# A hybrid linear-attention trunk: dropping the accumulating DMA in the second mixer, and loading the block it adds to by a DMA of its own elsewhere

## The chip, the cores and the metric

The kernel runs on one core of one Trainium2 chip. A core has five instruction streams that run side by side: TensorE (PE: matrix products, with its weight loads listed as PEld), VectorE (DVE), ScalarE (ACT), GpSimd (POOL) and SyncE (SP, which here only issues DMAs). Sixteen DMA engines move data between the HBM and the on-chip memory SBUF; products land in the eight banks of PSUM. The metric is the device time of one launch in microseconds (us), lower is better.

## The reference, cut to what matters

The reference is a trunk of two pre-norm residual layers in float32 on 256 tokens of width 2048: layer 0 mixes tokens by an HGRN2 gated recurrence, layer 1 by gated linear attention (GLA). Each mixer shares one input projection with a cross-attention into 256 memory tokens, and each layer ends with a SwiGLU network of inner width 5632.

```python
for layer in range(DEPTH):                       # DEPTH = 2
    hn = _rmsnorm(h, norm_mix[layer])
    if layer % NUM_MIXERS == 0:
        y, xq = _hgrn2_mixer(hn, hgrn_w_in[j], lbs[j], hgrn_onorm[j])
    else:
        y, xq = _gla_mixer(hn, gla_w_in[j], gla_w_gk[j], gla_b_gk[j], gla_onorm[j])
    xa = _memory_attention(xq, mem_n, w_mem_kv[layer])
    h = h + jnp.concatenate([y, xa], axis=-1) @ w_out[layer]
    hn = _rmsnorm(h, norm_ffn[layer])
    gate, up = jnp.split(hn @ w_gate_up[layer], 2, axis=-1)
    h = h + (jax.nn.silu(gate) * up) @ w_down[layer]
```

Nearly all of the work is in the weight products: `hn @ w_in`, `@ w_out`, `@ w_gate_up` and `@ w_down`, with `mem_n @ w_mem_kv` ahead of them. Each weight is used once, so each is loaded once.

## The kernel before, in words

**A product in three passes.** Each float32 factor is split into a high part that the PE takes at full rate and a low part, the rest (`split`, L276). ACT writes the high part, DVE (or, for a few, POOL at L292) subtracts it from the value to get the low part. A product is then three matmuls: high by high, high by low, low by high.

**Seven products for eight.** The weights of a product come in pairs of 128-row blocks, and two column ranges c0 and c1 are done together, so a pair is a 2 by 2 block matrix. It is loaded into one tile `raw` of four quarters, 128 partitions by up to 512 columns each: quarters 0 and 3 are the two row blocks of c0, quarters 1 and 2 are the two row blocks of c1. `raw` has three buffers. A pair of kind "S" is multiplied by a Strassen-Winograd scheme with seven block products (`seven`, L427); a pair of another kind takes eight. For "S" the kernel needs sums of quarters: quarter 1 plus quarter 2, then that sum minus quarter 0 (first `tt`, L436), then quarters 2 and 3 each minus the result (second `tt`, L437). Quarter 0, and quarters 2 and 3, are split before those two instructions, and their outcomes after them.

**Who makes the first sum.** `load_pair` (L413) issues, on SP's queue, a DMA for quarters 1 and 2 together (c1) and then a DMA for quarters 0 and 3 together (c0). For an "S" pair it then issues a third DMA on POOL's queue, which reads the second row block of c1 from HBM again and adds it into quarter 1 (`accum_op=ALU.add`, L425). That DMA may start only when the first has landed, and the first `tt` waits for it.

**Stages, in order of time.** Memory keys and values (`m0`, `m1`), HGRN (its projections `hx`, then for each of three groups `hf` and `hv`), output projection (`wo`), feed-forward (`f` and `fd`), then GLA (`gx`, `gk0`, `gg00`, `gg01`, `gk1`, `gg10`, `gg11`), output projection and feed-forward again. `project_two` (L522) runs the pairs of a mixer, of `w_out`, of `w_mem_kv` and of the end of `w_down`; `project_halves` (L597) those of `w_gate_up`. In GLA a product is 384 columns wide (two heads of 192, or one of 384), so a quarter is 192 KB; elsewhere it is 512 columns and 256 KB. GLA has ten "S" pairs: one in each of the two `gk` products ("------S-") and two in each of the four `gg` products ("-----SS-"). Their `raw` tiles have the numbers 230, 237, 238, 245, 246, 254, 261, 262, 269 and 270; names such as `parts230a` in the trace are the split parts of such a tile.

**What sets the order.** In the feed-forward stage the order on PE, DVE and ACT is the order in which the program writes it (`Engine.kept`, L141 and L614), with evictions and transposes put in at due times. In the other stages a planner, which estimates how long instructions and transfers take, fixes each engine's order at build time; small pieces of work such as the scores of a chunk, transposes and the decays are handed to it between pairs (`later`, `step`). On the chip every engine then works through its list in that order: an instruction whose input is late holds up all that stand behind it on its engine. When a product is done, DVE adds up its seven or eight banks (`early`, L552, and L594).

Of the kernel before, what the change touches and what calls it, by code (L numbers as in the profile page):

```python
# [14 lines left out]
ALU = mybir.AluOpType  # L15
# [25 lines left out]
def trunk_kernel(ctx: ExitStack, tc: tile.TileContext, x, mem, norm_mix, norm_ffn, norm_mem,  # L41
# [125 lines left out]
    def held(behind, func, *args):  # L167

        for e, last in behind:
            e.hold = last  # L170
        return func(*args)
# [7 lines left out]
    def mark(key):  # L179
        while waiting and waiting[0][0] <= key:  # L180
            waiting.pop(0)[2]()
# [228 lines left out]

    TIMES = {"S": (1,) * 7, "O": (0, 2, 2, 2, 2, 0, 0), "H": (0, 2, 2, 2, 1, 0, 1)}

    def load_pair(raw, w, p, c0, c1, n, kind):  # L413

        if n_w[0] == 1:
            for k, j, c in ((0, 0, c0), (0, 1, c1), (1, 3, c0), (1, 2, c1)):
                nc.sync.dma_start(out=raw[:, j, 0:n], in_=w[(2 * p + k) * P:(2 * p + k + 1) * P, c:c + n])
                if k == 0 and c == c1:
                    load_mem(0, 256, 512)
            return  # L420
        for j, c in ((slice(1, 3), c1), (slice(0, 4, 3), c0)):
            nc.sync.dma_start(out=raw[:, j, 0:n],
                              in_=w[2 * p * P:(2 * p + 2) * P, c:c + n].rearrange("(k p) c -> p k c", p=P))
        if kind == "S":
            nc.gpsimd.dma_start(out=raw[:, 1, 0:n], in_=w[(2 * p + 1) * P:(2 * p + 2) * P, c1:c1 + n], accum_op=ALU.add)  # L425

    def seven(i, raw, between=None):  # L427

        n = raw.shape[2]
        tt = ve.tensor_tensor  # L430
        b00, = split(raw[:, 0:1, :], f"{i}a")
        b11, b10 = split(raw[:, 2:4, :], f"{i}b")
        if between:
            between()

        tt(out=raw[:, 0, :], in0=raw[:, 1, :], in1=raw[:, 0, :], op=ALU.subtract)  # L436
        tt(out=raw[:, 2:4, :], in0=raw[:, 2:4, :], in1=raw[:, 0:1, :].broadcast_to([P, 2, n]), op=ALU.subtract)  # L437
        t6, t7 = split(raw[:, 0:2, :], f"{i}c", turned=True)
        t5, t4 = split(raw[:, 2:4, :], f"{i}d")
        return {1: ("x00", b00), 2: ("x01", b10), 3: ("z", b11), 4: ("x11", t4), 5: ("s", t5), 6: ("u", t6), 7: ("d0", t7)}  # L440
# [79 lines left out]
            self.x = lambda k, t: quads[p // 2].x(p % 2 * 2 + k, t)  # L520

    def project_two(pairs, plan, w, c0, c1, n, name, give, view=lambda ps: ps, onto=None, prep=None, behind=None,  # L522
                    base=0):

        ps, out = {}, []  # L530
        if any(c.isdigit() for c in plan):
            order, plan = [base + int(c) for c in plan[::2]], plan[1::2]
        else:
            sevens, plains = iter(range(len(PAIRS))), iter(range(plan.count("S"), len(PAIRS)))
            order = [next(sevens if c == "S" else plains) for c in plan]
        left = {b: plan.count("S") * (b < 8) + 2 * plan.count("-") * (b in (2, 3, 4, 8)) for b in range(1, 9)}

        def product(b, left_factor, right):
            first = b not in ps
            if first:  # L540
                ps[b] = bank(f"{name}p{b}")
            left[b] -= 1
            (xh, xl), (hi, lo) = left_factor, right
            acc = ps[b][:, 0:n]
            pe.matmul(acc, xh, hi, start=first, stop=False)
            pe.matmul(acc, xh, lo, start=False, stop=False)
            pe.matmul(acc, xl, hi, start=False, stop=left[b] == 0)

        def add(to, b, other):
            ve.tensor_tensor(out=to, in0=view(ps[b][:, 0:n]), in1=other, op=ALU.add)  # L550

        def early():  # L552
            l, r = give()
            out.extend((l(0), l(1), r(0), r(1)))
            s0, s1, e1, e0 = out
            ac.copy(out=s0, in_=view(ps[1][:, 0:n]))
            add(e1, 6, s0)
            add(s1, 7, e1)
            add(e0, 5, s1)
            add(e1, 5, e1)  # L560
            if onto:
                for to, part in zip(onto, out):
                    ve.tensor_tensor(out=to, in0=to, in1=part, op=ALU.add)
                out[:] = onto

        for at, (p, kind) in enumerate(zip(order, plan)):
            i, raw = new_raw()
            if i == 0:
                load_pair(raw, w, p, c0, c1, n, kind)
            if prep:  # L570
                prep(at)
            if i > 0:
                load_pair(raw, w, p, c0, c1, n, kind)
            if kind == "S":
                todo = held(behind, seven, i, raw[:, :, 0:n]) if behind else seven(i, raw[:, :, 0:n])
                last = at == plan.rindex("S")
                for b in (1, 6, 7, 5, 2, 4, 3) if last else (3, 2, 1, 6, 7, 5, 4):
                    product(b, pairs[p].get(todo[b][0]), todo[b][1])
                if last and at == len(plan) - 1:
                    early()  # L580
                elif len(pending) > MANY:
                    step()
                continue
            b00, b01 = split(raw[:, 0:2, 0:n], f"{i}a", 2 if i else 1)
            b11, b10 = split(raw[:, 2:4, 0:n], f"{i}b")
            if at > 0 and at == plan.rindex("S") + 1:
                early()
            for k, (lf, rt) in enumerate(((b00, b01), (b10, b11))):
                step()
                for b, t, right_factor in ((2, 0, lf), (4, 1, lf), (8, 1, rt), (3, 0, rt)):  # L590
                    if b == 8 and len(pending) > MANY:
                        step()
                    product(b, pairs[p].x(k, t), right_factor)
        for to, b in zip(out, (2, 4, 3, 8)):  # L594
            add(to, b, to)

    def project_halves(forms, kinds, w, c0, c1, name, key, keep):  # L597


        left = {b: sum(TIMES[kind][b - 1] for kind in kinds) for b in range(1, 8)}  # L600
        ps = {}

        def product(b, left_factor, right):
            first = b not in ps
            if first:
                ps[b] = bank(f"{name}p{b}")
            left[b] -= 1
            (xh, xl), (hi, lo) = left_factor, right
            pe.matmul(ps[b], xh, hi, start=first, stop=False)
            pe.matmul(ps[b], xh, lo, start=False, stop=False)  # L610
            pe.matmul(ps[b], xl, hi, start=False, stop=left[b] == 0)

        for p, kind in enumerate(kinds):
            Engine.kept = keep <= p  # L614
            i, raw = new_raw()
            load_pair(raw, w, p, c0, c1, 512, kind)
            x = forms[p].get
            last = p == len(PAIRS) - 1
            if kind == "S":
                todo = seven(i, raw, lambda: mark(key + p))  # L620
                for b in (1, 2, 6, 7, 5, 4, 3) if last else (1, 3, 2, 6, 7, 5, 4):
                    product(b, x(todo[b][0]), todo[b][1])
            else:
                b00, b01 = split(raw[:, 0:2, :], f"{i}a")
                mark(key + p)
                b11, b10 = split(raw[:, 2:4, :], f"{i}b")
                todo = [[(2, "x00", b00), (5, "x10", b01), (4, "x10", b00), (3, "d0", b01)]]
                if kind == "O":
                    todo.append([(2, "x01", b10), (5, "x11", b11), (4, "x11", b10), (3, "d1", b11)])
                else:  # L630
                    ve.tensor_tensor(out=raw[:, 3, :], in0=raw[:, 3, :], in1=raw[:, 2, :], op=ALU.subtract)
                    e1, = split(raw[:, 3:4, :], f"{i}c")
                    todo.append([(2, "x01", b10), (3, "x01", b11), (7, "x11", b11), (4, "x11", e1)])
                todo = [m for ms in zip(*todo) for m in ms] if last else todo[0] + todo[1]
                for b, f, right in todo:
                    product(b, x(f), right)
            step()
        return ps
# [398 lines left out]
    def gla_pair(w, pr, dec, decay, hq, r, yq):  # L1037
# [40 lines left out]
        def give():  # L1078
            for name in "kq":
# [2 lines left out]
            return [lambda t, d=d: d[:, t, :, 0:DK] for d in dst]  # L1082

        project_two(hq["pairs"], ("------S-", "------S-")[pr], w, kw + pr * 2 * DK, pr * 2 * DK, 2 * DK, f"gk{pr}", give,
                    lambda ps: ps.rearrange("p (a c) -> p a c", c=DK))
        for d in dst:
            for t in range(NT):
                ac.activation(out=d[:, t, :, 0:DK], in_=d[:, t, :, 0:DK], func=AF.Copy, scale=r[:, t:t + 1])
# [7 lines left out]
        for a in range(2):  # L1096
            def give():
                for dst, tag in ((gate, "gate"), (v, "v")):
# [1 line left out]
                return [lambda t, d=d[a]: d[:, t, :] for d in (gate, v)]  # L1100

            project_two(hq["pairs"], GLA[pr][a], w, 2 * kw + MIX + (2 * pr + a) * DV, 2 * kw + (2 * pr + a) * DV, DV,
                        f"gg{pr}{a}", give)
            for dst, func in ((gate[a], AF.Silu), (v[a], AF.Copy)):
                for t in range(NT):
                    ac.activation(out=dst[:, t, :], in_=dst[:, t, :], func=func, scale=r[:, t:t + 1])
# [288 lines left out]
```

## Time and profile before

| | |
|---|---|
| median of 3 runs | 2276.28 us (2270.11 to 2280.8) |
| the profiled execution | 2272.82 us, of it span 2271.0 us |
| granted TensorE clock | 0.999 |
| PE, PEld busy | 99%, 84% of the span |
| DVE, ACT, POOL busy | 87%, 63%, 9% |
| moved by DMA | 475.56 MB, 209 GB/s over the span |

A page of the profile has busy times by engine, the chain of work that ended last (followed back from the last instruction to what released each step), groups of equal instructions, and DMA issues with their size and the median time from issue to landing. A row of the timeline gives start, duration, engine, line, operation, `out<-in`, the number of instructions merged, and in brackets how long the engine had sat idle before it and what ended that. Matmuls are pipelined and their ends are modelled. Instructions of PE, DVE and ACT pass through one helper, so nearly all have line L151 and are told apart by their tiles.

### The profile page before, as it was taken

How to read it: one execution, taken by the hardware profiler on the slowest of the kernel's cores; microseconds unless marked ns; L12 is line 12 of the kernel's file. 1: busy time of each engine (PE TensorE's matmuls, PEld its weight loads, DVE VectorE, ACT ScalarE, POOL GpSimd, SP SyncE). 2: the span in 40 equal slices, each digit the busy share in tenths (PEclk: the TensorE clock that was granted, in tenths of full speed). 3: DMA queues.
4: the chain of work that ended last, by engine and by line, in shares of the span. 5: the costliest groups of instructions: out<-in, count | busy, mean ns of one | idle time of the engine just before them, and what ended most of it. 6: DMA issues, size and time to landing. Idle time of an engine off the chain costs nothing.

```text
span 2271.0 us, 30130 instructions
## 1 busy us (share of the span) xinstructions
PE 2247.5 (99%) x10710; PEld 1904.3 (84%) x10710; DVE 1974.3 (87%) x2449; ACT 1429.7 (63%) x1938; POOL 210.9 (9%) x215
## 2 busy tenths in 40 slices
PE   9999999999999999999999999999999999999998
PEld 7888888888888888888889899888888888888887
DVE  7889999898898889988996786789888898888997
ACT  7656656565666666666675565567566666666664
POOL 1000100000111111111100000000011111111110
PEclk9999999999999999999999999999999999999999
DMA  8656665656777777777765556466677777777774
GB/s 293 215 170 208 203 184 166 194 195 181 223 233 226 223 231 247 224 215 228 235 211 164 149 161 191 139 212 213 195 222 223 235 231 220 232 230 228 232 240 153
DMA packets 254827, 475.56 MB, mean 209 GB/s; under 512 B 15663, under 2 KB 46419, under 8 KB 254419
## 3 DMA queue, kind: packets, MB, share of 16 engines
q1 hardware_dynamic: 231203, 429.64, 56.1%
q0 software_dynamic: 22176, 39.72, 11.1%
q10 hardware_dynamic: 1296, 4.26, 0.5%
q8 instruction: 84, 1.38, 0.2%
q14 instruction: 68, 0.56, 0.1%
HBM read 470.42 MB, written 3.15 MB: 209 GB/s over the span
## 4 chain that ended last, share of the span: by engine, by line
PE 94%; DVE 2%; DMA 2%; issue 1%; ACT 0%; SPq 0%; POOL 0%; POOLq 0%; DVEq 0%; ACTq 0%
PE f_p L151 39%; PE fd L151 19%; PE wo L151 4%; PE m1p L151 2%; PE hv2p L151 2%; PE hv1p L151 2%; PE hv0p L151 2%; PE wo0p L151 2%; PE wo1p L151 2%; PE hf2p L151 2%; PE hf1p L151 2%; PE fd_0p L151 2%; PE m0p L151 2%; PE gg01p L151 1%; PE hf0p L151 1%; DMA raw<-in_gla_w_in_dram 1%
## 5 line engine op out<-in xcount | busy, mean ns | idle before, releaser
L151 DVE TENSOR_TENSOR raw<-raw 128x512 f32<-128x512 f32 (+3 forms) x320 | 299.0, 934 | 62.7 <-DMA raw<-in_w_gate_up_dram 34.0
L151 DVE TENSOR_TENSOR parts<-raw,parts 128x1024 fp32r<-128x1024 f32 (+1 forms) x196 | 224.3, 1179 | 23.4 <-ACT parts L151 23.0
L151 ACT CAST parts<-raw 128x1024 fp32r<-128x1024 f32 (+1 forms) x216 | 212.6, 1017 | 50.4 <-PE fd L151 6.5
L425 POOL DMA_DIRECT2D raw<-in_w_gate_up_dram x114 | 98.9, 867 | 990.2 <-DMA raw<-in_w_gate_up_dram 670.1
L151 ACT COPY h<-fd 128x512 f32<-128x512 f32 x80 | 46.6, 588 | 79.1 <-PE fd L151 75.8
L292 POOL TENSOR_TENSOR parts<-raw,parts 128x1024 fp32r<-128x1024 f32 x20 | 48.8, 2440 | 204.3 <-ACT parts L151 192.0
L151 ACT ACTIVATE s<-s,rf_r 128x512 f32<-128x512 f32 x44 | 31.8, 723 | 41.9 <-DVE s L151 41.7
L151 DVE TENSOR_TENSOR e<-f_p,e 128x512 f32<-128x512 f32 x66 | 45.3, 686 | 2.6 <-DVE s L151 0.5
L151 ACT COPY fd<-h 128x512 f32<-128x512 f32 x82 | 45.3, 585 | 0.0
L151 PE MATMUL fd<-parts,s_2h 128*128 128x512 f32 x128 | 39.8, 392 | 0.0
L151 PE MATMUL fd<-parts,s_0h 128*128 128x512 f32 x128 | 39.8, 392 | 0.0
L151 PE MATMUL fd<-parts,s_4h 128*128 128x512 f32 x128 | 39.8, 392 | 0.0
L151 PE MATMUL fd<-parts,s_8h 128*128 128x512 f32 x128 | 39.8, 392 | 0.0
L151 PE MATMUL fd<-parts,s_6h 128*128 128x512 f32 x128 | 39.8, 392 | 0.0
L151 PE MATMUL fd<-parts,s_3h 128*128 128x512 f32 x128 | 39.4, 389 | 0.0
L151 PE MATMUL fd<-parts,s_7h 128*128 128x512 f32 x128 | 39.4, 389 | 0.0
L151 PE MATMUL fd<-parts,s_5h 128*128 128x512 f32 x128 | 39.4, 389 | 0.0
L151 PE MATMUL fd<-parts,s_1h 128*128 128x512 f32 x128 | 39.4, 389 | 0.0
L151 DVE TENSOR_TENSOR s<-f_p,e 128x512 f32<-128x512 f32 x44 | 30.3, 690 | 10.1 <-PE f_p L151 8.2
L425 POOL DMA_DIRECT2D raw<-in_hgrn_w_in_dram x17 | 14.8, 872 | 216.0 <-DMA raw<-in_hgrn_w_in_dram 125.9
L151 DVE SCALAR_TENSOR_TENSOR s<-e,rf_r,s 128x512 f32<-128x512 f32 x44 | 31.0, 747 | 0.2
L151 PEld LDWEIGHTS fd<-parts,s_7h 128*128 128x128 f32 x128 | 24.0, 188 | 5.0
(5729 smaller groups left out, 7315.4 us busy)
## 6 DMA issues: line engine op xcount, KB each, us to landing
raw<-in_w_gate_up_dram SPq DMA_DIRECT2D x352, 512.0 KB, 4.2
raw<-in_w_down_dram SPq DMA_DIRECT2D x80, 1024.0 KB, 6.7
raw<-in_hgrn_w_in_dram SPq DMA_DIRECT2D x96, 512.0 KB, 4.2
raw<-in_gla_w_in_dram SPq DMA_DIRECT2D x96, 384.0 KB, 3.3
raw<-in_w_gate_up_dram POOLq DMA_DIRECT2D x114, 256.0 KB, 5.4
raw<-in_w_out_dram SPq DMA_DIRECT2D x16, 1024.0 KB, 5.2
raw<-in_w_out_dram SPq DMA_DIRECT2D x32, 512.0 KB, 4.1
raw<-in_w_mem_kv_dram SPq DMA_DIRECT2D x30, 512.0 KB, 5.6
```

The costliest lines, as they stand in the source:

```text
L151: ins = func(*args, **kwargs)
L292: low = (nc.gpsimd if free_port else ve).tensor_tensor(out=both[:, 1, k:j, 0:m], in0=src[:, k:j, :], in1=both[:, 0, k:j, 0:m].bitcast(F32) ...
L425: nc.gpsimd.dma_start(out=raw[:, 1, 0:n], in_=w[(2 * p + 1) * P:(2 * p + 2) * P, c1:c1 + n], accum_op=ALU.add)
```

## The change

`project_two` and `seven` get a flag `fed`, true by default, and GLA's two calls of `project_two` set it to false.

Where `fed` is false, an "S" pair has no accumulating DMA. Its load is the two DMAs on SP's queue, with c0 (quarters 0 and 3) now ahead of c1 (quarters 1 and 2), and `seven` adds quarter 2 into quarter 1 by one more DVE instruction in front of the two it had.

Where `fed` is true, an "S" pair has four DMAs instead of three: quarter 1 alone, the accumulating DMA on POOL's queue right behind it in the program, then quarters 0 and 3, then quarter 2 alone. Pairs of the other kinds keep two DMAs everywhere, with c0 now ahead of c1. The very first pair of the kernel is loaded as before.

```diff
-    def load_pair(raw, w, p, c0, c1, n, kind):
+    def load_pair(raw, w, p, c0, c1, n, kind, fed):
...
-        for j, c in ((slice(1, 3), c1), (slice(0, 4, 3), c0)):
-            nc.sync.dma_start(out=raw[:, j, 0:n],
-                              in_=w[2 * p * P:(2 * p + 2) * P, c:c + n].rearrange("(k p) c -> p k c", p=P))
-        if kind == "S":
-            nc.gpsimd.dma_start(out=raw[:, 1, 0:n], in_=w[(2 * p + 1) * P:(2 * p + 2) * P, c1:c1 + n], accum_op=ALU.add)
+        if kind == "S" and fed:
+            rows = [w[(2 * p + k) * P:(2 * p + k + 1) * P, c1:c1 + n] for k in range(2)]
+            nc.sync.dma_start(out=raw[:, 1, 0:n], in_=rows[0])
+            nc.gpsimd.dma_start(out=raw[:, 1, 0:n], in_=rows[1], accum_op=ALU.add)
+        nc.sync.dma_start(out=raw[:, 0:4:3, 0:n], in_=w[2 * p * P:(2 * p + 2) * P, c0:c0 + n].rearrange("(k p) c -> p k c", p=P))
+        if kind == "S" and fed:
+            nc.sync.dma_start(out=raw[:, 2, 0:n], in_=rows[1])
+        else:
+            nc.sync.dma_start(out=raw[:, 1:3, 0:n], in_=w[2 * p * P:(2 * p + 2) * P, c1:c1 + n].rearrange("(k p) c -> p k c", p=P))
...
-    def seven(i, raw, between=None):
+    def seven(i, raw, fed, between=None):
...
+        if not fed:
+            tt(out=raw[:, 1, :], in0=raw[:, 1, :], in1=raw[:, 2, :], op=ALU.add)
         tt(out=raw[:, 0, :], in0=raw[:, 1, :], in1=raw[:, 0, :], op=ALU.subtract)
...
         project_two(hq["pairs"], ("------S-", "------S-")[pr], w, kw + pr * 2 * DK, pr * 2 * DK, 2 * DK, f"gk{pr}", give,
-                    lambda ps: ps.rearrange("p (a c) -> p a c", c=DK))
+                    lambda ps: ps.rearrange("p (a c) -> p a c", c=DK), fed=False)
...
             project_two(hq["pairs"], GLA[pr][a], w, 2 * kw + MIX + (2 * pr + a) * DV, 2 * kw + (2 * pr + a) * DV, DV,
-                        f"gg{pr}{a}", give)
+                        f"gg{pr}{a}", give, fed=False)
```

More of the change, by code (lines that the diff above doesn't have):

```diff
@@ L522, in project_two @@
     def project_two(pairs, plan, w, c0, c1, n, name, give, view=lambda ps: ps, onto=None, prep=None, behind=None,
-                    base=0):
+                    base=0, fed=True):
         ps, out = {}, []
@@ L568, in project_two @@
             if i == 0:
-                load_pair(raw, w, p, c0, c1, n, kind)
+                load_pair(raw, w, p, c0, c1, n, kind, fed)
             if prep:
@@ L572, in project_two @@
             if i > 0:
-                load_pair(raw, w, p, c0, c1, n, kind)
+                load_pair(raw, w, p, c0, c1, n, kind, fed)
             if kind == "S":
-                todo = held(behind, seven, i, raw[:, :, 0:n]) if behind else seven(i, raw[:, :, 0:n])
+                todo = held(behind, seven, i, raw[:, :, 0:n], fed) if behind else seven(i, raw[:, :, 0:n], fed)
                 last = at == plan.rindex("S")
@@ L615, in project_halves @@
             i, raw = new_raw()
-            load_pair(raw, w, p, c0, c1, 512, kind)
+            fed = True
+            load_pair(raw, w, p, c0, c1, 512, kind, fed)
             x = forms[p].get
@@ L619, in project_halves @@
             if kind == "S":
-                todo = seven(i, raw, lambda: mark(key + p))
+                todo = seven(i, raw, fed, lambda: mark(key + p))
                 for b in (1, 2, 6, 7, 5, 4, 3) if last else (1, 3, 2, 6, 7, 5, 4):
```

## The prediction

> **What bounds the kernel now.** I read the page first (busy times, the chain that ended last, the DMA issues), then the busy times by stage, then the timeline of PE in the one stage where PE had gaps, and last the rows of DVE ahead of each gap.
>
> ```profile
> span 2271.0 us, 30130 instructions
> PE 2247.5 (99%) x10710; PEld 1904.3 (84%) x10710; DVE 1974.3 (87%) x2449; ACT 1429.7 (63%) x1938; POOL 210.9 (9%) x215
> ...
> PE 94%; DVE 2%; DMA 2%; issue 1%; ACT 0%; SPq 0%; POOL 0%; POOLq 0%; DVEq 0%; ACTq 0%
> ```
>
> PE is idle for 2271.0 − 2247.5 = 23.5 us in all. A change that leaves the matmuls alone, as this one does, can win no more than that. The rows by stage (window; length, then busy time of PE, PEld, DVE, ACT, POOL) say where these 23.5 us lie.
>
> ```profile
> 0.00:105.00 105.00, 101.51 (x475) 83.46 (x476) 80.96 (x116) 69.63 (x114) 9.43 (x13) 1.00 0.75 254
> ...
> 146.00:422.00 276.00, 275.98 (x1376) 232.72 (x1375) 260.30 (x358) 165.91 (x226) 19.91 (x22) 1.00 0.62 190
> ...
> 517.00:1164.00 647.00, 647.00 (x2904) 536.72 (x2903) 578.90 (x623) 417.81 (x516) 75.08 (x69) 1.00 0.74 226
> ...
> 1210.00:1484.00 274.00, 262.96 (x1601) 255.70 (x1600) 205.42 (x338) 160.74 (x257) 15.55 (x23) 0.99 0.56 166
> ...
> 1575.00:2222.00 647.00, 647.00 (x2904) 536.55 (x2903) 579.50 (x622) 418.61 (x517) 75.13 (x69) 1.00 0.74 226
> 2222.00:2271.00 49.00, 41.34 (x183) 33.91 (x181) 34.53 (x51) 21.94 (x35) 1.11 (x2) 0.97 0.43 151
> ```
>
> The HGRN groups (146 to 422) and both feed-forward stages have no PE gap at all. GLA (1210 to 1484) has 274.00 − 262.96 = 11.0 us, the largest part of the 23.5; of the rest 3.5 us lie at the start and 7.7 us at the end, where the last outputs are scaled and stored. So the change can win in GLA, and only there. Its PE gaps are these (the bracket is the idle time and what ended it):
>
> ```profile
> 1263.47 1.99 PE L151 MATMUL zp<-gk 128*128 128x256 f32 x8 [1.79 <-DVE gk L151]
> 1282.62 0.44 PE L151 MATMUL tgk<-ident,gsk 128*128 128x128 f32 x2 [1.03 <-ACT gsk L151]
> 1283.86 0.88 PE L151 MATMUL tgk<-ident,gsk 128*128 128x128 f32 x6 [0.80 <-ACT gsk L151]
> ...
> 1327.33 1.16 PE L151 MATMUL slg<-GQ 128*128 128x128 f32 x8 [2.34 <-DVE GQ L151]
> ...
> 1422.06 1.16 PE L151 MATMUL slg<-GQ 128*128 128x128 f32 x8 [2.39 <-ACT GQ L151]
> 1426.47 1.13 PE L151 MATMUL slg<-GQ 128*128 128x128 f32 x8 [1.15 <-DVE GQ L151]
> ...
> 1463.84 0.30 PE L151 MATMUL ty<-ident,ggate 128*128 128x128 f32 x1 [0.53 <-DVE gro_v L151]
> 1465.15 0.33 PE L151 MATMUL ty<-turned_id,ggate 128*128 128x128 f32 x1 [1.01 <-DVE ggate L151]
> ```
>
> They add up to 11.04 us, all of the stage's idle time.
>
> **GLA: what is removed.** Ten accumulating DMAs go. What they cost today is the idle time of DVE ahead of the first `tt` of a pair, the one that takes the sum. First the ten of them as a group (count, busy time, mean ns, idle time before them), then the ones that idled longest:
>
> ```profile
> L151 DVE TENSOR_TENSOR raw<-raw 128x384 f32<-128x384 f32 x10 | 5.6, 557 | 14.2 <-DMA raw<-in_gla_w_in_dram 10.1 <-issue 3.2 <-DVE parts237a L151 0.5
> ...
> 1255.19 0.51 ACT L151 CAST parts230a<-raw 128x384 fp32r<-128x384 f32 x1 [0.49 <-DMA raw<-in_gla_w_in_dram]
> 1260.45 0.56 DVE L151 TENSOR_TENSOR raw<-raw 128x384 f32<-128x384 f32 x1 [4.16 <-DMA raw<-in_gla_w_in_dram]
> ...
> 1262.99 0.42 DVE L151 COPY gk<-tlow 128x256 f32<-128x256 f32 x1
> ...
> 1410.70 0.56 DVE L151 TENSOR_TENSOR raw<-raw 128x384 f32<-128x384 f32 x1 [1.39 <-issue]
> ...
> 1418.13 0.56 DVE L151 TENSOR_TENSOR raw<-raw 128x384 f32<-128x384 f32 x1 [3.02 <-DMA raw<-in_gla_w_in_dram]
> ...
> 1457.89 0.56 DVE L151 TENSOR_TENSOR raw<-raw 128x384 f32<-128x384 f32 x1 [2.93 <-DMA raw<-in_gla_w_in_dram]
> ```
>
> Three of the PE gaps stand right behind these stalls. Pair 230: DVE stands still until 1260.45, and the copy of `gk` at 1262.99, for which PE waits at 1263.47, is behind it on DVE. Pairs 261 and 262: DVE idles 1.39 and 3.02 us, and the decays `GK` and `GQ`, for which PE waits at 1422.06 and 1426.47, are behind. Pair 269: DVE idles 2.93 us, and the normalisation `gro_v`, for which PE waits at 1463.84 and 1465.15, is behind.
>
> **GLA: what is added.** One DVE instruction for each of the ten pairs, two inputs and one output of 128x384 float32. The group above is this very kind of instruction: 557 ns, so 10 × 0.557 = 5.6 us of DVE time against 14.2 us of idle time that goes or shrinks. SP's count of DMAs stays, and c0 and c1 change places. The first work on a pair, the cast of quarter 0, needs c0, which now is in front; the new sum needs c1, which now comes last, at about the moment at which c0 came before. For pair 230 that is just before 1255.19, where ACT had waited for it; DVE was free from 1260.45 − 4.16 = 1256.29. So the sum starts at once and its data is no new wait.
>
> **GLA: the sum.** For each place: the stall that goes less the added instructions, but no more than the PE gap behind it.
> - Pair 230: 4.16 − 0.56 = 3.60 us saved on DVE, the gap is 1.79 us. Win 1.79.
> - Pairs 261 and 262: 1.39 + 3.02 − 2 × 0.557 = 3.30 us saved, the gaps are 2.39 + 1.15 = 3.54 us. Win 3.30.
> - Pair 269: 2.93 − 0.56 = 2.37 us saved, the gaps are 0.53 + 1.01 = 1.54 us. Win 1.54.
> - Pairs 237 and 238, ahead of the gap at 1327.33: nearly no stall there to remove (0.5 us, the group row's `parts237a`), two instructions added, 1.11 us. Of the 13 us ahead of that gap DVE idles in the two places below, 1.9 us together, and both times for an ACT result that itself follows on DVE's or PE's work, so between 0 and 1.11 us reaches PE. I take the middle, 0.55. Loss 0.55.
>
> ```profile
> 1314.11 1.23 DVE L151 TENSOR_TENSOR GF<-GF,ab 128x1024 f32<-128x1024 f32 x1 [1.11 <-ACT ab L151]
> ...
> 1318.45 0.96 DVE L151 TENSOR_TENSOR parts239a<-raw,parts239a 128x768 fp32r<-128x768 f32 x1 [0.77 <-ACT parts239a L151]
> ```
>
> - Pairs 245, 246 and 254: no gap behind them; hidden by PE, which has work ready there. If that cover were gone: 3 × 0.557 = 1.7 us.
> - The gaps at 1282.62 and 1283.86 are the adding up of the finished `gk` banks on DVE; no load is in front of it, so they stay.
>
> Together 1.79 + 3.30 + 1.54 − 0.55 = 6.1 us faster. Bounds: nothing is won below 0 if the loads are what DVE waits for (a rival, below); above, all eight gaps, 11.0 us.
>
> **Elsewhere: 144 pairs with one more DMA.** The issues (count, KB each, median us from issue to landing):
>
> ```profile
> raw<-in_w_gate_up_dram SPq DMA_DIRECT2D x352, 512.0 KB, 4.2
> raw<-in_w_down_dram SPq DMA_DIRECT2D x80, 1024.0 KB, 6.7
> ...
> raw<-in_w_gate_up_dram POOLq DMA_DIRECT2D x114, 256.0 KB, 5.4
> ...
> raw<-in_hgrn_w_in_dram POOLq DMA_DIRECT2D x17, 256.0 KB, 4.2
> ...
> raw<-in_w_out_dram POOLq DMA_DIRECT2D x6, 256.0 KB, 4.0
> ...
> raw<-in_w_down_dram POOLq DMA_DIRECT2D x4, 256.0 KB, 7.1
> ...
> raw<-in_w_mem_kv_dram POOLq DMA_DIRECT2D x3, 256.0 KB, 5.6
> ```
>
> 114 + 17 + 6 + 4 + 3 = 144 pairs. Two sizes give a line: 512 KB more cost 6.7 − 4.2 = 2.5 us, so a DMA has about 4.2 − 2.5 = 1.7 us that do not depend on its size, and 256 KB should land in 4.2 − 1.25 = 2.95 us. The accumulating DMA can thus start about 1.25 us earlier and the sum is there about that much earlier (as an estimate; between 0, if POOL is held up otherwise, and 4.2 − 1.7 = 2.5). This shortens waits of DVE that PE does not see: where PE has no gap, the gain is nothing. The cover is PE's queue of finished work, and it is deep:
>
> ```profile
> 904.65 0.69 DVE L151 TENSOR_TENSOR parts160a<-raw,parts160a 128x512 fp32r<-128x512 f32 x1 [2.82 <-ACT parts160a L151]
> ...
> 915.03 0.61 PE L151 MATMUL f_p<-parts160a,hf_0h 128*128 128x512 f32 x2
> ...
> L422 SPq DMA_DIRECT2D raw<-in_w_gate_up_dram x352: 367/368/1781, 496.1 to 2177.9; - x176
> ```
>
> DVE was done with `parts160a` at 905.34, PE took it at 915.03: 9.7 us of lead. On the other side of the ledger, quarter 2 now leaves last, one issue later than c0 did: 0.37 us by the last row, with the accumulating DMA perhaps beside it on the DMA engines. SP's queue gets 144 × 0.37 = 53 us of issue time spread over the span, and behind those issues stand only later loads. I take 0 us for all of this; the bounds are 0 for a gain (no PE gap to close) and the rival on the third DMA for a loss. Pairs of other kinds swap c0 and c1, but their first split takes quarters 0 and 1 together and so needs both DMAs, as before: 0.
>
> **The total.** 2272.82 − 6.1 = 2266.7 us for a run like the profiled one. That one stands 2276.28 − 2272.82 = 3.5 us below the median of the three runs, so the median after should be 2276.28 − 6.1 = 2270.2, rounded to 2270.
>
> **Rivals.**
> *Hidden anyway (the loads, not the accumulating DMAs, hold DVE).* If c1, now last, lands late, DVE waits at the new sum instead of at the old one. For: ACT itself waited for c0 of pair 230 until 1255.19. Against: DVE then stood 4.16 us longer. If two thirds of the stalls stay, 2 us are won: 2274.
>
> *All gaps close.* The planner decides GLA's order anew with ten late transfers gone and may put the adding up and the decays earlier; then up to 11.0 us: 2265. Against: the gaps at 1282.62 and 1327.33 hang on finished banks and on DVE's load, which gets 5.6 us more.
>
> *The planner's order gets worse.* Outside the feed-forward stages, changed estimates of 30 loads with four DMAs (HGRN, output, memory) and ten in GLA move DVE instructions. DVE is busy 260.30 of 276 us in HGRN, so there is little room. If one gap of the size at 1327.33 opens in each of the three groups and two more elsewhere, 5 × 2.34 = 11.7 us are lost against 6.1 won: 2282.
>
> *Slower: the third DMA's fixed 1.7 us is not overlapped.* The place is the feed-forward stages, whose DVE order is fixed: if quarter 2 lands late, the split of quarters 2 and 3 waits and all DVE work behind it. DVE has (647.00 − 578.90) + (647.00 − 579.50) = 135.6 us of idle time there, 1.19 us for each of the 114 pairs. From 1.19 us of lateness for each pair on, PE pays; at the full 1.7 us it is (1.7 − 1.19) × 114 = 58 us, so 2328 after the win in GLA. Against it: DMAs on one queue overlap. In GLA the two loads of pair 230 were both there by 1255.19, though each is 384 KB.
>
> On this the Trainium skill speaks against the change ("DMA: Bandwidth & Descriptors", section "Anatomy of one DMA — SWDGE (gpsimd) path"): a DMA, there one issued by GpSimd, has a constant part of about 2.0 us, mostly the wait until its last write is confirmed, so that many small ones cost more than few large ones. The 1.7 us worked out above agree. By that rule with nothing overlapped, the loss would be (2.0 − 1.19) × 114 = 92 us; the lead of PE and the overlapping loads are why I do not go by it.
>
> **How the numbers follow.** Chances: forecast (3.5 to 9 us won) 0.58; hidden anyway 0.16; all gaps close 0.09; worse order 0.12; third DMA 0.05. The runs of before spread over 2270.11 to 2280.8, about ±0.25% around the median, so less than 0.5% (11.4 us) can't well be told from no change; that is where "same" ends. Faster than 2264.9 needs nearly all gaps closed, or the forecast and a low draw of the runs: 0.12. Slower than 2287.7 needs the third DMA, or a worse order that loses half as much again: 0.07. The rest, 0.81, is the same. The range takes in the forecast, the first two rivals and the worse order with half the spread of the runs (about 4 us) at either end: 2260 to 2283; the third DMA is left out. The likeliest case alone would be 2264 to 2276.
>
> **What would show each step.** The profile after should have no accumulating DMA from `gla_w_in`, and 20 DVE instructions `raw<-raw` of 128x384 with an idle time before them of a few us instead of 14.2. The PE waits for `gk`, for `GQ` behind pairs 261 and 262 and for `gro_v` should be gone or under 0.5 us each; the wait for `GQ` near 1327 should be there still, perhaps longer; GLA's PE idle time should fall from 11.0 to about 5 us. The feed-forward stages should take 647 us as before with no PE gap, and DVE's waits for `gate_up` loads should shrink. I am wrong if GLA keeps its stalls at the new sum, if a feed-forward stage grows, or if HGRN shows PE gaps.

## The result, and the profile after

The changed kernel takes 2262.16 us (median of 6 runs, 2260.94 to 2262.71), the kernel before 2273.2 us (median of 6, 2270.11 to 2280.8). The ratio is 0.9943 with a 95% interval of 0.9933 to 0.9953: faster by 0.47 to 0.67%. The prediction said 2270 us (2260 to 2283), a win of 6.1 us; the win is 11.0 us by these medians.

The page of the changed kernel (span, busy times, chain that ended last), beside which the prediction's first fence stands for the kernel before:

```profile
span 2259.0 us, 30203 instructions
...
PE 2245.2 (99%) x10710; PEld 1903.1 (84%) x10710; DVE 1974.4 (87%) x2459; ACT 1425.3 (63%) x1938; POOL 202.3 (9%) x205
...
PE 94%; DVE 2%; issue 1%; DMA 1%; ACT 0%; SPq 0%; POOLq 0%; DVEq 0%; POOL 0%; ACTq 0%
```

The span is 12.0 us shorter, and PE idles 2259.0 − 2245.2 = 13.8 us instead of 23.5. Nearly all of this difference of 9.7 us lies in GLA. The next two fences are the busy times by stage (window; length, busy time of PE, PEld, DVE, ACT, POOL with their instruction counts, then granted clock, DMA share, GB/s). GLA is measured from the first `gx` matmuls to the first of `wo`, before and after:

```profile
1208.43:1483.79 275.36, 264.32 (x1613) 257.10 (x1613) 206.62 (x340) 162.04 (x260) 15.55 (x23) 0.99 0.55 165
```

```profile
146.00:422.00 276.00, 275.98 (x1376) 232.76 (x1375) 259.62 (x358) 166.01 (x226) 19.05 (x21) 1.00 0.62 189
517.00:1164.00 647.00, 647.00 (x2904) 536.55 (x2903) 574.44 (x616) 415.12 (x514) 74.30 (x69) 1.00 0.74 225
1562.00:2210.00 648.00, 648.00 (x2908) 537.36 (x2908) 575.83 (x617) 416.27 (x514) 74.52 (x69) 1.00 0.74 225
...
1208.56:1471.54 262.98, 261.49 (x1613) 255.78 (x1613) 210.69 (x350) 162.22 (x260) 6.81 (x13) 1.00 0.52 165
```

The same 1613 matmuls take 262.98 us instead of 275.36, 12.4 us less. Of these, 9.55 are idle time of PE (275.36 − 264.32 = 11.04 against 262.98 − 261.49 = 1.49). The other 2.83 us lie in PE's busy time, at an unchanged number of matmuls; the granted clock of the stage reads 0.99 before and 1.00 after. HGRN and both feed-forward stages run without a gap, as before.

PE's waits in GLA after the change, and the DVE instructions on `raw`, now 20 (count, busy time, mean ns, idle time ahead of them):

```profile
1280.25 0.44 PE L151 MATMUL tgk<-ident,gsk 128*128 128x128 f32 x2 [0.59 <-ACT gsk L151]
1281.49 0.88 PE L151 MATMUL tgk<-ident,gsk 128*128 128x128 f32 x6 [0.80 <-ACT gsk L151]
```

```profile
L151 DVE TENSOR_TENSOR raw<-raw 128x384 f32<-128x384 f32 x20 | 11.1, 555 | 0.2 <-DMA raw<-in_gla_w_in_dram 0.2
```

Of eight gaps two are left, both from adding up the `gk` banks. The idle time of DVE ahead of the sums fell from 14.2 to 0.2 us. But the wait for `GQ` near 1327, which the prediction had left standing and a little longer, is gone too.

Outside GLA the loads of the changed kernel look like this (count, KB, median us from issue to landing):

```profile
raw<-in_w_gate_up_dram SPq DMA_DIRECT2D x238, 512.0 KB, 4.8
...
raw<-in_w_gate_up_dram SPq DMA_DIRECT2D x228, 256.0 KB, 4.0
...
raw<-in_w_gate_up_dram POOLq DMA_DIRECT2D x114, 256.0 KB, 5.3
```

The row of 256 KB mixes two loads: quarter 1 alone, which is the first load of its pair, and quarter 2 alone, which is the last. (A landing is known only for about a quarter of SP's loads, those that the trace can match with their issue.) The views of the two lines of the program keep them apart, first quarter 1, then quarter 2 (each landing is over all 144 loads of its line):

```profile
L423 SPq DMA_DIRECT2D raw<-in_w_gate_up_dram x114: 340/341/341, 495.7 to 2165.5; - x114
...
DMA to landing us min/median/max: 2.6/2.8/5.4
```

```profile
L427 SPq DMA_DIRECT2D raw<-in_w_gate_up_dram x114: 459/467/1459, 496.6 to 2166.4; - x114
...
DMA to landing us min/median/max: 3.9/4.6/6.9
```

So the own DMA for quarter 1 lands after 2.8 us, where the load of two quarters before, also the first of its pair, took 4.2. By the issue times of the 114 `gate_up` pairs, POOL issues the accumulating DMA 3.4 us after the pair's first load instead of 4.5 us (medians), and its sum has landed 9.5 us after that first load instead of 10.3 us.

### The profile page after: what moved, and what is told of

Same layout as the page of the kernel before. It is cut to its first block, busy times and chain, and to the rows that moved or that the text cites. A ratio compares the mean times of both kernels' runs of the same rounds, so it can differ in the third digit from the quotient of the medians.

```text
span 2259.0 us, 30203 instructions
## 1 busy us (share of the span) xinstructions
PE 2245.2 (99%) x10710; PEld 1903.1 (84%) x10710; DVE 1974.4 (87%) x2459; ACT 1425.3 (63%) x1938; POOL 202.3 (9%) x205
## 4 chain that ended last, share of the span: by engine, by line
PE 94%; DVE 2%; issue 1%; DMA 1%; ACT 0%; SPq 0%; POOLq 0%; DVEq 0%; POOL 0%; ACTq 0%
PE f_p L151 37%; PE fd L151 17%; PE wo L151 4%; PE m1p L151 2%; PE hv2p L151 2%; PE hv1p L151 2%; PE hv0p L151 2%; PE hf0p L151 2%; PE wo0p L151 2%; PE wo1p L151 2%; PE hf2p L151 2%; PE hf1p L151 2%; PE m0p L151 2%; PE gk0p L151 1%; PE gk1p L151 1%; PE gg11p L151 1%
## 5 line engine op out<-in xcount | busy, mean ns | idle before, releaser
L151 DVE TENSOR_TENSOR raw<-raw 128x512 f32<-128x512 f32 (+3 forms) x330 | 303.7, 921 | 49.8 <-DMA raw<-in_w_gate_up_dram 30.9
L151 PEld LDWEIGHTS fd<-parts,s_1h 128*128 128x128 f32 x128 | 24.0, 188 | 5.0
```

The lines of the kernel that those rows point to most:

```text
L151: ins = func(*args, **kwargs)
```

## The experiments

The order in which DVE and ACT work through GLA is not the same in the two kernels: the planner changed it along with the loads. In the two traces, by operation and tiles and without the new sums, 57 of DVE's 339 positions in GLA differ, 24 of ACT's 260 and none of PE's; in HGRN none differ. So the first two experiments part the loads from the order.

**New loads, old order.** Edit: after all instructions are issued, edges without a wait chain DVE's and ACT's GLA instructions in the order of the kernel before (271 positions on DVE, 190 on ACT, and the ten new sums each right ahead of its user). In the trace DVE's order is that of before, position for position.

```diff
+    for names in ORDER:
+        for a, b in zip(names, names[1:]):
+            tc.add_manual_dep(made[f"I-{b}"], f"I-{a}", mybir.DependencyInfo(
+                mybir.DependencyClass.NoSync, mybir.DependencyReason.DATA), reason="order")
```

> The changed kernel with the order of VectorE and ScalarE in the second mixer pinned to the order of the kernel before (each new sum right ahead of the instruction that uses it). Theory S (the stalls at the accumulating DMA are what went): the PE waits for gk, for GQ behind pairs 261 and 262 and for gro_v go, the wait for GQ near 1327 stays at 2 to 4 us; 8 to 10 us faster than before (0.9956 to 0.9965). Theory O (the planner's new order is what won): most waits of before stay; within 4 us of before (0.998 to 1.0).

Measured: 2264.67 us against 2275.15 for the kernel before beside it, ratio 0.9955 (0.9943 to 0.9968). PE's waits in GLA (in this copy the helper is at L187):

```profile
1280.44 0.44 PE L187 MATMUL tgk<-ident,gsk 128*128 128x128 f32 x2 [0.59 <-ACT gsk L187]
1281.67 0.88 PE L187 MATMUL tgk<-ident,gsk 128*128 128x128 f32 x6 [0.80 <-ACT gsk L187]
...
1323.47 1.16 PE L187 MATMUL slg<-GQ 128*128 128x128 f32 x8 [2.43 <-DVE GQ L187]
...
1418.89 1.13 PE L187 MATMUL slg<-GQ 128*128 128x128 f32 x8 [0.17 <-DVE GQ L187]
```

The gaps that the prediction tied to the accumulating DMAs go with them, the one near 1327 stays, at 2.43 instead of 2.34 us. Theory S holds for most of the gain, and that one gap belongs to the order. The win is at the upper end of what theory S expected, just past it (0.9955 against 0.9956, well within the interval).

**Old loads, new order.** The same edges in the kernel before, with the order of the changed kernel.

> The kernel before, accumulating DMAs and all, with the order of VectorE and ScalarE in the second mixer pinned to that of the changed kernel. Theory S: only the wait for GQ near 1327 goes, the stalls at the accumulating DMA stay; 1 to 4 us faster than before (0.998 to 0.9995). Theory O: 8 to 12 us faster (0.9947 to 0.9965).

Measured: 2269.93 us, ratio 0.9981 (0.9973 to 0.9990).

```profile
1263.88 1.99 PE L186 MATMUL zp<-gk 128*128 128x256 f32 x8 [1.40 <-DVE gk L186]
...
1324.99 1.16 PE L186 MATMUL slg<-GQ 128*128 128x128 f32 x8 [0.33 <-DVE GQ L186]
...
1420.16 1.16 PE L186 MATMUL slg<-GQ 128*128 128x128 f32 x8 [1.63 <-ACT GQ L186]
...
L186 DVE TENSOR_TENSOR raw<-raw 128x384 f32<-128x384 f32 x10 | 5.6, 558 | 13.4 <-DMA raw<-in_gla_w_in_dram 8.9 <-issue 3.1 <-DVE scg L186 1.0
```

The gap near 1327 shrinks to 0.33 us. DVE's idle time at the sums stays at 13.4 us, and with it the gaps behind pairs 230, 262 and 269; the second gap of 1.15 us behind pair 262 is gone. The ratio is within what theory S expected, though the medians differ by 5.2 us. So the order alone wins some 0.2%, the loads alone some 0.45%. PE's idle time in GLA adds up better than the times do. These are the rows of GLA, with the new loads and the old order, then with the old loads and the new order:

```profile
1208.78:1474.26 265.48, 261.49 (x1614) 255.69 (x1613) 211.36 (x350) 162.23 (x260) 6.82 (x13) 1.00 0.52 163
```

```profile
1209.22:1480.69 271.47, 262.90 (x1613) 255.53 (x1613) 205.38 (x340) 161.70 (x260) 15.58 (x23) 1.00 0.56 167
```

Of the 11.04 us of idle time before, 3.99 are left with the new loads alone and 8.57 with the new order alone: 7.05 and 2.47 us less, together 9.52, where both at once took 9.55 away.

**Only the second mixer.** Edit to the changed kernel: where `fed` is true, the loads of before.

```diff
+        if fed:
+            for j, c in ((slice(1, 3), c1), (slice(0, 4, 3), c0)):
...
+            if kind == "S":
+                nc.gpsimd.dma_start(out=raw[:, 1, 0:n], ..., accum_op=ALU.add)
+            return
```

> Only the second mixer's part of the change; all other loads as before. Both theories: as fast as the whole change (0.9935 to 0.995). Rival F (the earlier sums elsewhere win something too): slower than the whole change by 2 us or more (above 0.9952).

Measured: 2260.88 us, ratio 0.9938 (0.9926 to 0.9951). The order on DVE and ACT in GLA is that of the changed kernel, position for position. The whole gain is there; the changed loads elsewhere add nothing to it that the runs can tell.

**Only elsewhere.** Edit: the changed kernel with the loads of before where `fed` is false, the accumulating DMA included, and without the new sum.

> Only the loads outside the second mixer are changed (144 pairs with one more DMA, c0 ahead of c1 elsewhere). Theories S and O: as before, 0.9990 to 1.0010, because PE has no gap there. Rival F: 0.998 or less. Rival of the third DMA's fixed cost: 1.005 or more.

Measured: 2274.97 us, ratio 0.9996 (0.9987 to 1.0005). 144 more DMAs cost nothing and win nothing beyond the interval, about 0.1% either way. Rival F and the third DMA's fixed cost fall.

**An own DMA everywhere, no new sums.** Edit: the two `fed=False` taken out.

> The changed kernel with the accumulating DMA kept in the second mixer too, behind a DMA of its own for quarter 1, as elsewhere; no new sums on VectorE. If the stalls are the accumulating DMA's late landing, an earlier start shortens them by 0.5 to 1.5 us each and they do not go: 2 to 6 us faster than before (0.9974 to 0.9991), the idle time ahead of the first sum of the ten pairs between 4 and 11 us instead of 14. If only giving the work to VectorE helps: 0.9990 to 1.0005. If the early DMA is all it takes: as the whole change, 0.9935 to 0.995.

Measured: 2272.91 us against 2275.39, ratio 0.9990 (0.9981 to 0.9999).

```profile
L151 DVE TENSOR_TENSOR raw<-raw 128x384 f32<-128x384 f32 x10 | 5.6, 557 | 17.3 <-DMA raw<-in_gla_w_in_dram 17.3
...
raw<-in_gla_w_in_dram SPq DMA_DIRECT2D x86, 384.0 KB, 3.9
...
raw<-in_gla_w_in_dram SPq DMA_DIRECT2D x20, 192.0 KB, 3.2
...
raw<-in_gla_w_in_dram POOLq DMA_DIRECT2D x10, 192.0 KB, 3.8
```

DVE's idle time at the sums did not fall to between 4 and 11 us, as expected; it is 17.3 us, within the 14.2 to 18.4 us of three profiles of the kernel before. The 3.2 us of the quarters are a median of three known landings, of quarters 1 and 2 together, so they say little. The issue times say more: POOL issues the ten accumulating DMAs 3.2 us after the pair's first load instead of 4.0 us (medians), and each then needs its 3.8 us as before (3.7). Loading the block first, by a DMA of its own, does not cure the stalls; taking the accumulating DMA away does. The time, 0.1% lower, lies where the bands of two of the three expectations meet.

**No sum.** It leaves out the addition of quarter 2 into quarter 1.

```diff
-        if not fed:
-            tt(out=raw[:, 1, :], in0=raw[:, 1, :], in1=raw[:, 2, :], op=ALU.add)
```

> The changed kernel without the ten new sums on VectorE: it leaves out the addition of quarter 2 into quarter 1 in the second mixer, so its time holds the transfers of the change without the 5.6 us of VectorE work. If PE hides these sums, as the prediction took for all but 0.55 us: within 1 us of the whole change. If they are paid in full: 5 to 6 us faster than the whole change.

Measured: 2263.38 us, ratio 0.9948 (0.9936 to 0.9961), no faster than with the sums. It is 1.2 us above the whole change, just outside "within 1 us", with overlapping intervals. The planner orders this version differently again, and a wait for `GQ` of 1.18 us stands near 1324, so the price of the sums alone is not parted from the order here.

**Three sums.** Each of the ten sums is issued three times, so this version computes another product.

```diff
-        if not fed:
+        for _ in range(0 if fed else 3):
             tt(out=raw[:, 1, :], in0=raw[:, 1, :], in1=raw[:, 2, :], op=ALU.add)
```

> The changed kernel with each of the ten sums issued three times (quarter 2 is added three times, another product): 20 more VectorE instructions of 0.557 us, 11.1 us. If PE's lead hides VectorE's work away from the places where it runs without pause: 1 to 4 us slower than the whole change, with PE gaps again behind pairs 237, 238, 261, 262 and 269. If VectorE's work in this stage counts in full: 11 us slower.

Measured: 2262.35 us, ratio 0.9942 (0.9927 to 0.9958), as fast as the change with one sum each. Neither 1 to 4 nor 11 us were lost.

```profile
1314.11 0.61 PE L151 MATMUL gg00p<-parts238c,hm_1m 128*128 128x384 f32 x2 [0.29 <-ACT parts238c L151]
1315.15 0.44 PE L151 MATMUL gg00p<-parts238d,hm_1m 128*128 128x384 f32 x1 [0.25 <-ACT parts238d L151]
...
L151 DVE TENSOR_TENSOR raw<-raw 128x384 f32<-128x384 f32 x40 | 22.1, 554 | 0.2
```

DVE does 11.0 us more of this work, and besides the two gaps of the `gk` banks PE waits 0.54 us in all, for the split of pair 238 behind the sums. The planner ordered this version with the added sums in it: 103 of DVE's 339 other positions differ from the changed kernel's. So in an order planned for them, 30 sums of 0.55 us (16.6 us) are hidden by PE's lead in this stage, as long as no DMA holds DVE up; in a given order this was not tried.

**c1 first.** Edit: for the ten pairs, the two loads in their old order, c1 ahead of c0.

> The changed kernel with c1 loaded ahead of c0 for the ten pairs of the second mixer, as before. If the order of the two loads does not matter, as predicted: within 1 us of the whole change. If c0 in front is part of the gain: 2 us or more slower.

Measured: 2264.52 us, ratio 0.9953 (0.9939 to 0.9966). The medians differ by 2.4 us, the intervals overlap. The profile leans towards c0 in front as a part of the gain:

```profile
L151 DVE TENSOR_TENSOR raw<-raw 128x384 f32<-128x384 f32 x20 | 11.1, 556 | 5.0 <-DMA raw<-in_gla_w_in_dram 4.6
...
1294.72 2.46 PE L151 MATMUL spg<-GQ,GK 128*128 128x128 f32 x16 [2.25 <-DVE GQ L151]
```

DVE idles 5.0 us at the sums instead of 0.2, and one PE gap of 2.25 us is there, with a fall of the granted clock behind it (1.7 us lost, as told below). In this version too the planner moved DVE instructions (39 of 339 positions differ from the changed kernel's), so how much is the landing and how much the order was not parted. With c1 first the kernel still wins 0.5%: most of the gain does not need c0 in front.

**The kernel before, twice more.** The runs of the kernel before spread over 10 us, those of the changed kernel over 2. The 2.83 us of PE's busy time led to the granted clock:

> The kernel before, unchanged, profiled once more. Theory C (behind PE gaps the granted clock sometimes falls to half for some 3 us, at about 1.7 us each, and this makes most of the spread of its runs): GLA keeps the same gaps within 0.3 us, and the span is 2269.3 us plus 1.7 us for each such fall in the profile. Rival: the stage's length varies by the gaps themselves or by transfers, with no fall of the clock.

> The same again, for another draw of the same quantity: a span of 2269.3 us plus 1.7 us for each fall of the granted clock (theory C), or a span that does not go with the number of falls (rival).

Measured: spans of 2275.1 and 2275.9 us. The lost time was summed over windows of 5 us, each counted by one minus its granted clock, without the end of the program where PE has run out of work. The profiled run of before lost 1.7 us in this way, the two others 3.4 and 5.15. From 2269.3 us on, which is the first span less its 1.7 us, theory C then says 2271.0, 2272.7 and 2274.5 us; the last two were 2.4 and 1.4 us longer than that. The count is rather too high: 0.95 of the 3.4 us lie in a window in which PE was busy for 0.87 of 5 us. The gaps were not the same within 0.3 us either. The first of the two:

```profile
1297.83 0.56 DVE L151 TENSOR_TENSOR raw<-raw 128x384 f32<-128x384 f32 x1 [2.62 <-DMA raw<-in_gla_w_in_dram]
...
1301.77 1.16 PE L151 MATMUL slg<-GQ 128*128 128x128 f32 x8 [1.95 <-ACT GQ L151]
...
1425.05 2.08 PE L151 MATMUL slg<-GQ 128*128 128x128 f32 x8 [4.18 <-ACT GQ L151]
...
L151 DVE TENSOR_TENSOR raw<-raw 128x384 f32<-128x384 f32 x10 | 5.6, 558 | 18.4 <-DMA raw<-in_gla_w_in_dram 10.0 <-issue 7.7 <-DVE parts270a L151 0.7
...
1418.00:1436.00 18.00, 13.82 (x73) 13.50 (x72) 13.48 (x24) 5.98 (x9) 0.00 (x0) 0.81 0.29 87
```

So theory C is half right: falls of the clock add to the spread, and so do the stalls themselves, which vary from run to run (14.2 us of DVE idle time in the prediction's profile, 18.4 here, 17.3 in the third). A PE gap near 1301, of which that profile had nothing, was 1.95 us here, behind a stall of 2.62 us at the first sum of pair 237, where that profile had 0.46. The other profiles of kernels with the ten accumulating DMAs (the third one of before, old loads with the new order, only elsewhere, an own DMA everywhere) have this gap too, at 0.78 to 1.94 us; no profile without them has it at these matmuls.

## Why the prediction was right, and where it was too small

**The number: inside the range, outside the forecast case.** The case that had 0.58, 3.5 to 9 us won, did not come; 11.0 us were won, and 2262.16 us is below the 2264.9 us that were to be passed with a chance of 0.12. Of the 8.0 us between 2270.2 and 2262.16, 3.1 are the base (2276.28 us was a median of three runs, 2273.2 us is one of six) and 4.9 are the win. That the range held the outcome is owed to its low end, set for "all gaps close" and half the spread of the runs, and so in part to luck.

**What bounds, and where a gain can lie: right.** PE bounds, only GLA has room, and only GLA moved (second mixer alone 0.9938, elsewhere alone 0.9996).

**Pairs 230, 261, 262 and 269, 6.6 us: right.** In the kernel with the new loads and the old order the waits for `gk` and for `gro_v` are gone and those for `GQ` behind pair 262 are down from 3.54 to 0.17 us.

**Pairs 237 and 238, a loss of 0.55 us: wrong in sign.** The step kept the planner's order for the sum and gave a change of order to two rivals. In the old order the gap is 2.43 us with the two added instructions, where three profiles of before have 2.27 to 2.34: a cost of some 0.1 us, below the middle that was taken. In the new order the gap is gone. "Nearly no stall there to remove" was true of the one profile that was read and of few others: at pair 237 DVE stood 2.39 to 3.10 us in the two other profiles of before, with an own DMA everywhere and with only the loads elsewhere changed, and the gap near 1301 behind it was 1.32 to 1.95 us there. So this pair had a gain in it that the sum took for a loss. In this stretch the list of DVE in the changed kernel has `GQ` ahead of `parts242a`; before:

```profile
1325.72 0.96 DVE L151 TENSOR_TENSOR parts242a<-raw,parts242a 128x768 fp32r<-128x768 f32 x1
1326.59 0.69 DVE L151 TENSOR_TENSOR GQ<-GQ,Tg 128x512 f32<-128x512 f32 x1
```

and after:

```profile
1320.01 0.69 DVE L151 TENSOR_TENSOR GQ<-GQ,Tg 128x512 f32<-128x512 f32 x1
...
1324.46 0.95 DVE L151 TENSOR_TENSOR parts242a<-raw,parts242a 128x768 fp32r<-128x768 f32 x1
```

That the order closes the gap is shown by both pinned kernels; which of its moves does it was not tried one by one.

**The gaps of the `gk` banks: nearly right.** "They stay" was 1.83 us; 1.39 are left.

**What the sum had no term for: PE's busy time.** 2.83 of the 12.4 us. That a change which leaves the matmuls alone can win no more than PE's idle time was thus not quite so. 1.7 us of it is a fall of the granted clock behind the gap at 1282, by windows of 5 us before and after:

```profile
1280.00:1285.00 5.00, 3.17 (x21) 2.61 (x20) 5.00 (x11) 3.05 (x6) 0.00 (x0) 1.00 0.61 193
1285.00:1290.00 5.00, 5.00 (x24) 4.90 (x23) 2.78 (x6) 3.55 (x7) 0.00 (x0) 0.66 0.75 225
```

```profile
1277.00:1282.00 5.00, 3.61 (x23) 3.05 (x22) 5.00 (x13) 2.42 (x5) 0.00 (x0) 1.00 0.73 245
1282.00:1287.00 5.00, 5.00 (x35) 4.96 (x34) 3.73 (x8) 4.85 (x10) 0.31 (x1) 1.00 0.59 169
```

5 × (1 − 0.66) = 1.7 us. The remaining 1.1 us goes with the old loads and not with the clock: with the old loads and the new order PE is busy 262.90 us in GLA at a clock of 1.00, with the new loads and the old order 261.49, as after the change. It would fit the modelled ends of the matmuls ahead of each gap, which make a gap look shorter than it is; the weight loads give longer gaps at the same places (2.11 us for 1.79 at pair 230). That is argued, not shown, and the gap of 2.43 us with the new loads and the old order, which adds nothing to PE's busy time, speaks against it.

So, by terms, in us: 1.79 + 3.54 + 1.54 for the pairs with stalls, 2.34 for the gap near 1327, 0.44 for the `gk` banks, 2.83 in busy time, less 0.10 in small waits, make 12.4. The prediction had 6.1.

**The base.** The sum was taken from a profile with the least stall and one fall of the clock, and its 6.1 us were then taken off the median. The other two profiles show that longer runs had longer stalls in GLA and more falls of the clock, which the change removes along with the rest. That the spread of the runs was part of what could be won is a step the prediction did not take.

**Elsewhere: zero right, and the mechanism nearly so.** 256 KB were to land in 2.95 us from a line through 512 and 1024 KB; quarter 1 took 2.8. The accumulating DMA was to start about 1.25 us earlier and its sum to come as much earlier; they did so by 1.1 and 0.8 us. The idle time ahead of DVE's work on `raw` that ends with a `gate_up` transfer went from 34.0 to 30.9 us, by the costliest groups of the pages before

```profile
L151 DVE TENSOR_TENSOR raw<-raw 128x512 f32<-128x512 f32 (+3 forms) x320 | 299.0, 934 | 62.7 <-DMA raw<-in_w_gate_up_dram 34.0
```

and after:

```profile
L151 DVE TENSOR_TENSOR raw<-raw 128x512 f32<-128x512 f32 (+3 forms) x330 | 303.7, 921 | 49.8 <-DMA raw<-in_w_gate_up_dram 30.9
```

The rival with the third DMA's fixed cost did not occur: both feed-forward stages are still without a PE gap.

**c0 and c1 change places at no cost: open.** The median with c1 first says that c0 in front is worth some 2.4 us, the intervals do not part them.

**The rivals.** The outcome is nearest to "all gaps close" (2265 at 0.09) and below the likeliest case's own 2264 to 2276. In us won it equals that rival's 11.0; by PE's idle time 9.55 of 11.0 us went, and the two gaps of the `gk` banks stayed, as the prediction had said. Its mechanism, the planner's new order, did come and took 2.47 us of idle time. It should have had more weight, since the prediction knew that the planner orders this stage by the very transfers that were taken away.

## What to carry to other kernels

An accumulating DMA makes a chain of two transfers, and an in-order engine that waits for its end holds up everything behind it; ten instructions of 0.56 us on an engine with slack were cheaper than ten such waits, and three times as many, in an order planned for them, cost no more. Where a planner orders the work by estimates, taking a transfer away also changes the order, so price the move with both and pin the order to tell them apart. One profile of such a stage is one draw: the stall at pair 237 was 0.46 us in the one that was read and 2.4 to 3.1 us in others, so read a second one before pricing a stall at nothing. A stage with gaps on PE varies from run to run, by the stalls and by the clock behind them; closing the gaps narrows the runs too (10.7 to 1.8 us here).

## What was not expected of the hardware

**The clock falls behind short gaps.** In the profiled run of before PE idles 1.83 us of the 5 us from 1280 on, and in the window behind it the granted clock is 0.66 over 5 us. In another profile of the same kernel, with the same gap at that place, it did not fall there; it fell behind a gap of 4.18 us near 1425. None of the three profiles whose GLA gaps all stay under 0.9 us (the change, the second mixer only, three sums) shows a fall there. The length of a gap alone does not decide it: of the nine PE gaps of 2.2 to 2.5 us in the profiles' GLA stages, four have a fall of 1.5 to 1.7 us behind them and five have none. The Trainium skill ("TensorE: Matmul & The Clock Gate", "Why this matters for your kernels") says to avoid idle gaps of more than about 3 us between bursts of matmuls, as one idle window of activity halves the clock. The halving agrees: the window from 1286 to 1288 reads 0.50, and 1.7 us lost is 3.4 us at half speed. The gap that it takes was shorter here, 1.03 and 0.80 us within 2 us.

**A load's place in the row counts as much as its size.** In the changed kernel 256 KB landed after 2.8 us where the load was the first of its pair (L423) and after 4.6 us where it was the last (L427). In GLA 384 KB took 3.3 us before, where the landings known are all of first loads, and 3.9 us after, where they are all of loads behind another one. A median over both places, such as the 4.0 us of all 256 KB loads, hides this.
